# Feeding the filling work of the attention pipelines by an estimate of how far VectorE and ScalarE are behind TensorE

## The chip, the cores and the metric

The kernel runs on one core of one Trainium2 chip, as one launch. The metric is the device time of that core in microseconds (us). Engines are named PE (TensorE), DVE (VectorE), ACT (ScalarE), POOL (GpSimd) and SP (SyncE, which here issues transfers).

## The reference

Two layers of a transformer block over 512 image tokens `x` and 256 context tokens `z`, width 1024, everything in float32. Cut to what matters:

```
def hybrid_layer(x, z, c, c_ctx, p, ...):
    mod_x = silu(c) @ p['w_ada'] + p['b_ada']       # six vectors of 1024: shift, scale, gate, twice
    mod_z = silu(c_ctx) @ p['w_ada'] + p['b_ada']
    hx, hz = x * (1 + sc1x) + sh1x, z * (1 + sc1z) + sh1z
    mix_x, mix_z = token_mixers(hx, hz, ...)
    x = layer_norm(ALPHA * x + g1x * mix_x)
    x = layer_norm(ALPHA * x + g2x * sq_relu_mlp(x * (1 + sc2x) + sh2x))
    ...                                             # z likewise, in the first layer only

def token_mixers(hx, hz, p, ...):                   # three branches, each with its own projections
    ya = retention_branch(...)   # 4 heads, two directions, silu gates g_fwd and g_bwd
    yb = na_branch(...)          # neighbourhood attention, 8 heads
    yc = mla_branch(...)         # latent attention, 8 heads
    y = sigmoid(g0) * (ya @ w_branch_ret) + sigmoid(g1) * (yb @ w_branch_na) + sigmoid(g2) * (yc @ w_branch_mla)
    return y @ p['w_out']
```

The second layer returns only `x`, so it has no context outputs there.

## The kernel before, in words

Every float32 product is made of three matmuls on a high and a low part (`mm3`). So each weight, fetched as a block of 128 x 1024, is first split: ACT writes the high part (`hi_of`, L383), DVE the low part of the first 512 columns and POOL that of the other 512 (`lo_of`, L386). Weights rotate through three buffers, the projections' results through three PSUM banks (`pd`).

The program order of a layer is: MLA pipeline, neighbourhood attention pipeline (Natten), retention pipeline of the first two heads (`ret.run(0)`), all filling work that is left (`fill.rest()`), retention pipeline of the other two heads (`ret.run(1)`), together with two branch projections, then the third branch projection, the output projection, layer norm, and the MLP in eight parts. In the first layer the output projection goes in two rounds, `z` first and then `x`. The compiler's scheduler may move an instruction ahead of others on its engine, but on PE the instructions stand close to program order.

`pipeline(items, lags, want)` walks the attention items in stages: scores and softmax (s0), transposes (s1), weighted values (s2). After each stage it calls `fill.feed(want / 3)`, which gives credit in us of PE time and advances generators of other work until the credit is used up. A generator yields after each piece and says how much PE time it holds (`cost`, columns / 2400). A piece can be larger than the credit; then the credit is negative and nothing is fed until it has been earned back. `Fill` has two queues: `urgent` is work that the next item needs (keys and queries of the next head, the projections and values of Natten, the preparation of a retention pair), and `jobs` is work that is needed only later: `ret_gates` (24 tiles of 256 columns in the first layer, 16 in the second, in four groups that share two weights) and `gate_tiles` (24 weights, each for a tile of 512 columns and in the first layer one of 256 too). `feed` takes from `urgent` first. `finish(gen)` runs a generator to its end, without credit, when its result is needed.

A third stream hangs on the first. `later` (class `Paced`) holds the modulation vectors that are not yet there: 80 blocks of `w_ada`, each fetched (512 KB) and then multiplied and summed by DVE, once for `x` and once for `z` (L500). Its instructions are pinned behind the DVE instruction that stands before them in program order. It advances by a rate per us of other work:

```
fill.after = lambda c: later.step(c * ADA_GATES)    # L1665, 0.3 for each us that fill.rest() feeds
later.step(c * ADA_BRANCH)                          # L1689, 0.05 in the third branch
later.until(1 + 8)                                  # L1710, before the output projection
later.step(ADA_OUT)                                 # L1735, 0.3 for each weight after the third
later.until(1 + 24)                                 # L1737, before the layer norm of each round
```

The first advance only fetches, so `until(1 + 8)` stands for eight blocks: the vector that scales the output projection's results (L1719). The next sixteen scale and shift the layer norm's result. In the MLP the rate is 1.1 for each weight.

Of the kernel before, what the change touches and what calls it, by code (L numbers as in the profile page):

```python
# [42 lines left out]
WANT = ((4.0, 2.5, 6.0, 8.0), (4.0, 2.5, 6.0, 8.0))  # L43

RET_LAGS = ((0, 1, 3), (0, 1, 2))

NA_AHEAD = 2

# [11 lines left out]
class Units:  # L60


    def __init__(self):
        self.index = {}
        self.blocks = []
# [172 lines left out]
class Fill:  # L238
# [2 lines left out]

    def __init__(self):
        self.urgent = []
        self.jobs = []
        self.credit = 0.0
        self.after = None

    def step(self):  # L250
        for queue in (self.urgent, self.jobs):
            while queue:
                c = next(queue[0], None)
                if c is not None:
                    if self.after:
                        self.after(c)
                    return c
                queue.pop(0)
        return None

    def feed(self, want):
        self.credit += want
        while self.credit > 0:
# [3 lines left out]
                return  # L267
            self.credit -= c

    def finish(self, gen):  # L270
        if gen in self.urgent:
            self.urgent.remove(gen)
        for _ in gen:
            pass

    def rest(self):
        while self.step() is not None:
            pass


class Pending:
# [31 lines left out]
def block_kernel(ctx, tc, xT, zT, cond, wu, sp, bias, tab, out):  # L313
    nc = tc.nc
# [32 lines left out]
    def bank_d():  # L347

        return ps_d.tile([128, 512], F32, tag="pd", name=nm("pd"))
# [26 lines left out]
    def R(ap):  # L376
        return ap.bitcast(F32R)

    act, dve, pool, pe, sync = nc.scalar, nc.vector, nc.gpsimd, nc.tensor, nc.sync
    fill, pend = Fill(), Pending()  # L380

    def hi_of(dst, src, scale=1.0):
        act.activation(R(dst), src, AF.Copy, scale=scale)  # L383
# [25 lines left out]
    dve.memset(ones, 1.0 / D)  # L409


    def load(*key, spare=False):
        raw = dbl("wraw") if spare else wraw.tile([128, 1024], F32, tag="wraw", name=nm("wraw"))
        fetch_in(raw, wu[IDX[key]])
        return raw

    def weight(*key, own=False, spare=False, w_dve=W_DVE):
        raw = load(*key, spare=spare)
        if own:
            w = (dbl("w"), dbl("w"))  # L420
        else:
            t = wsp.tile([128, 2, 1024], F32, tag="wsp", name=nm("wsp"))
            w = (t[:, 0], t[:, 1])
        hi_of(w[0], raw)
        for eng, cols in ((dve, slice(0, w_dve)), (pool, slice(w_dve, 1024))):
            if cols.start < cols.stop:
                lo_of(w[1][:, cols], raw[:, cols], w[0][:, cols], eng)
        return w
# [273 lines left out]

        return s0, s1, s2

    def pipeline(items, lags, want, tick=None):

        n = len(items)
        for t in range(n + lags[-1]):  # L710
            for s, lag in enumerate(lags):
                if 0 <= t - lag < n:
                    items[t - lag][s]()
                fill.feed(want / len(lags))
            if tick:
                tick(t)

# [419 lines left out]
    def ret_gates(l, hx, hz, need, store):  # L1137
# [5 lines left out]
        for p2 in range(2):  # L1143
            for dr, name in enumerate(("gf", "gb")):
                wg = [weight(l, name, p2, j) for j in range(2)]
                for i, lhs in enumerate(tiles):
                    p = bank_d()[:, :256]
                    token_major(p, lhs, wg, 4, KT)
                    g = ft("gt")[:, :256]
                    act.activation(g, p, AF.Tanh, scale=0.5)  # L1150
                    dve.scalar_tensor_tensor(g, g, 1.0, p, ALU.add, ALU.mult)
                    sync.dma_start(store[p2, i][dr], g)
                    yield cost(24 * 256)

    class Retention:
# [260 lines left out]

        def run(self, p2, want):
            items = [self.item(p2, o, c) for o in range(2) for c in range(3 if self.need else 2)]
            pipeline(items, RET_LAGS[p2], want)


    def gate_tiles(l, groups, store):
# [446 lines left out]
```

## Time and profile before

| | us |
|---|---|
| timed runs: median of 3 (lowest to highest) | 2669.43 (2669.32 to 2672.81) |
| the profiled execution, device time | 2672.0 |
| its span, first to last instruction | 2670.0 |
| PE busy in the span | 2524.7 (95%) |
| DVE busy in the span | 1801.6 (67%) |

The span is what the trace covers; some 2 us lie around it. Stages are given as stretches of the span, in us from its start: MLA 115 to 410, Natten 410 to 607, `ret.run(0)` 607 to 687, what `fill.rest()` and the last credit of `ret.run(0)` feed 687 to 787, `ret.run(1)` and the branches 787 to 912, the output projection 912 to 989, all in the first layer; and MLA 1636 to 1880, Natten 1880 to 2049, `ret.run(0)` 2049 to 2114, the rest of the filling 2114 to 2160, in the second. Neighbouring stages overlap by a few us. "PE busy" of a stretch counts a matmul to its modelled end, so the time without a busy PE is the stretch less that number. PEclk is the granted share of TensorE's 2.4 GHz; 0.5 is 1.2 GHz.

### The profile page before, as it was taken

The numbers are of one execution on the slowest core, as the hardware profiler recorded it, in microseconds if no ns is written. First come the engines' busy times: TensorE is split into PE (matmuls) and PEld (weight loads), VectorE is DVE, ScalarE is ACT, GpSimd is POOL, SyncE is SP. The second block draws the span as 40 slices with busy tenths as digits, with TensorE's granted clock in tenths as the row PEclk, the third lists the DMA queues.
The fourth block names the chain that finished last, engine by engine and source line by source line (L and its number), as shares of the span: only waits on it lengthen the run. The fifth ranks groups of instructions, "written<-read, shape, count | busy, mean of one in ns | idle before, by whom it ended". The sixth has DMA issues, their size and how long they took to land. (4 is left out here: it accounts for less than half of the span.)

```text
span 2670.0 us, 40740 instructions
## 1 busy us (share of the span) xinstructions
PE 2524.7 (95%) x15218; PEld 2241.1 (84%) x15218; DVE 1801.6 (67%) x3326; ACT 1157.5 (43%) x2176; POOL 1048.8 (39%) x816
## 2 busy tenths in 40 slices
PE   6999999997999898999999989999999899999997
PEld 4899998987888787888888878888888788888887
DVE  8565556676978894767777775566568758734357
ACT  4555545563323345222222345555556434632225
POOL 6312113345335655222222452222334557743334
PEclk8999999999999999999999999999999999999999
DMA  6222223423665543344444423332342356433333
GB/s 237 72 87 83 72 85 95 141 78 98 237 205 153 191 127 103 111 133 125 134 134 122 133 83 114 96 96 88 117 149 91 103 185 206 127 111 95 98 100 119
DMA packets 143001, 329.48 MB, mean 123 GB/s; under 512 B 16978, under 2 KB 54738, under 8 KB 142804
## 3 DMA queue, kind: packets, MB, share of 16 engines
q1 hardware_dynamic: 132436, 311.15, 37.7%
q10 hardware_dynamic: 10368, 15.73, 1.6%
q8 instruction: 120, 1.97, 0.3%
q14 instruction: 77, 0.63, 0.1%
HBM read 288.27 MB, written 36.45 MB: 122 GB/s over the span
## 5 line engine op out<-in xcount | busy, mean ns | idle before, releaser
L432 PE MATMUL pd<-op,wsp 128*128 128x512 f32 (+1 forms) x3080 | 1074.8, 350 | 38.6 <-DVE ms L1492 8.4
L433 PE MATMUL pd<-op,wsp 128*128 128x512 f32 (+1 forms) x3080 | 1073.0, 348 | 14.6 <-DVE op L386 8.4
L434 PE MATMUL pd<-op,wsp 128*128 128x512 f32 (+1 forms) x3080 | 1069.3, 347 | 7.1 <-DVE wsp L386 7.1
L386 POOL TENSOR_TENSOR wsp<-wraw,wsp 128x512 fp32r<-128x512 f32 x317 | 522.3, 1650 | 988.3 <-ACT wsp L383 874.3
L432 PEld LDWEIGHTS pd<-op,wsp 128*128 128x128 f32 x3080 | 588.6, 192 | 115.8 <-ACT op L588 10.0
L433 PEld LDWEIGHTS pd<-op,wsp 128*128 128x128 f32 x3080 | 590.2, 192 | 87.7 <-DVE op L386 12.3
L434 PEld LDWEIGHTS pd<-op,wsp 128*128 128x128 f32 x3080 | 589.3, 191 | 80.1 <-DVE wsp L386 9.4
L383 ACT ACTIVATE wsp<-wraw 128x1024 fp32r<-128x1024 f32 x319 | 336.2, 1055 | 391.5 <-PE pd L434 271.1
L386 DVE TENSOR_TENSOR wsp<-wraw,wsp 128x512 fp32r<-128x512 f32 (+1 forms) x319 | 283.3, 889 | 190.7 <-ACT wsp L383 184.7
L647 PE MATMUL pd<-wsp,op 128*128 128x256 f32 x704 | 203.1, 289 | 2.5 <-DVE pr L757 2.0
L649 PE MATMUL pd<-wsp,op 128*128 128x256 f32 x704 | 201.3, 286 | 0.2 <-POOL wsp L386 0.2
L648 PE MATMUL pd<-wsp,op 128*128 128x256 f32 x704 | 201.1, 286 | 0.0
L500 DVE CUSTOM_DVE_ANT_0 cond<-graw,cond,sp 128x1024 bf16<-128x1024 f32 x112 | 167.5, 1495 | 43.3 <-DMA graw<-wu 42.8
L1756 DVE TENSOR_TENSOR rl<-rl 128x256 f32<-128x256 f32 (+1 forms) x104 | 68.6, 659 | 138.9 <-ACT rl L1755 138.6
L386 DVE TENSOR_TENSOR pt<-pst,pt 128x512 fp32r<-128x512 f32 (+1 forms) x208 | 121.3, 602 | 48.2 <-ACT pt L383 46.4
L647 PEld LDWEIGHTS pd<-wsp,op 128*128 128x128 f32 x704 | 137.1, 195 | 3.6 <-issue 2.8
L649 PEld LDWEIGHTS pd<-wsp,op 128*128 128x128 f32 x704 | 136.6, 194 | 0.8 <-POOL wsp L386 0.4
L648 PEld LDWEIGHTS pd<-wsp,op 128*128 128x128 f32 x704 | 137.0, 195 | 0.1
L1770 DVE TENSOR_TENSOR t<-pd,t 128x512 f32<-128x512 f32 (+1 forms) x132 | 80.4, 613 | 77.6 <-PE pd L434 77.4
L1755 ACT ACTIVATE rl<-pd 128x256 f32<-128x256 f32 (+1 forms) x104 | 51.6, 496 | 174.3 <-PE pd L434 174.2
L616 PE MATMUL pso<-pt,t 128*128 128x256 f32 x704 | 115.3, 293 | 10.7 <-DVE ntx L623 4.0
L383 ACT ACTIVATE pt<-pst 128x512 fp32r<-128x512 f32 (+1 forms) x208 | 104.8, 529 | 46.4 <-PE pst L599 39.8
(284 smaller groups left out, 3925.8 us busy)
## 6 DMA issues: line engine op xcount, KB each, us to landing
wraw<-wu SPq DMA_DIRECT2D x327, 512.0 KB, 3.7
graw<-wu SPq DMA_DIRECT2D x56, 512.0 KB, 3.7
ada<-wu SPq DMA_DIRECT2D x40, 512.0 KB, 5.7
gg<-gate ACTq DMA_DIRECT2D x48, 256.0 KB, 2.0
gl<-gg SPq DMA_DIRECT2D x48, 256.0 KB, 3.6
zbias<-bias SPq DMA_DIRECT2D x64, 128.0 KB, 2.3
t<-vd SPq DMA_DIRECT2D x28, 256.0 KB, 5.4
gd<-gt SPq DMA_DIRECT2D x40, 128.0 KB, 2.4
```

The lines of the kernel that those rows point to most:

```text
L383: act.activation(R(dst), src, AF.Copy, scale=scale)
L386: (eng or dve).tensor_tensor(R(dst), src, hi, op=ALU.subtract)
L432: pe.matmul(ps, R(a[0]), R(b[0]), start=start, stop=False)
L433: pe.matmul(ps, R(a[0]), R(b[1]), start=False, stop=False)
L434: pe.matmul(ps, R(a[1]), R(b[0]), start=False, stop=stop)
L500: i = dve.tensor_tensor_reduce(cs[2], raw, cs[t], 0.5, spt[l][:, SP_BADA + c : SP_BADA + c + 1], ALU.mult, ALU.add, mods[l][:, c, t : t + 1])
L616: pe.matmul(o, R(vts[k]), R(pts[k]), start=k == 0, stop=k == n - 1)
L647: pe.matmul(ps, R(a[0]), R(w[0][:, o : o + 256]), start=k == 0, stop=False)
L648: pe.matmul(ps, R(a[1]), R(w[0][:, o : o + 256]), start=False, stop=False)
L649: pe.matmul(ps, R(a[0]), R(w[1][:, o : o + 256]), start=False, stop=k == nk - 1)
L1756: dve.tensor_tensor(t, t, t, op=ALU.mult)
L1770: dve.tensor_tensor(a, ps, a, op=ALU.add)
```

## The change

Operations on ACT, DVE, POOL and PE are counted as the program is written out: `Metered` adds to `Load` a duration worked out from the columns of the operation's output, and `Load` keeps for each engine the time at which it would be through, with a start no earlier than 1.0 us (`EARLY`) before PE's own time. `behind()` is how far the later of ACT and DVE is past PE. After each stage of a pipeline, `fill.level()` advances generators of `jobs` (not `urgent`, and without credit) as long as `behind()` is over 2.0 us (`LEAD`). `ret.run(1)` has no levelling. While a group of `ret_gates` is unfinished (`holding`), `feed` too takes from `jobs` alone, and `finish` completes the group first. The function `load` is renamed `raw_weight`, since its name is used for the estimate.

```
--- before.py
+++ after.py
@@ -43,6 +43,8 @@
 WANT = ((4.0, 2.5, 6.0, 8.0), (4.0, 2.5, 6.0, 8.0))
 
 RET_LAGS = ((0, 1, 3), (0, 1, 2))
+
+LEAD, EARLY = 2.0, 1.0
 
 NA_AHEAD = 2
 
@@ -241,14 +243,17 @@
 
 
 
-    def __init__(self):
+    def __init__(self, load):
         self.urgent = []
         self.jobs = []
         self.credit = 0.0
         self.after = None
-
-    def step(self):
-        for queue in (self.urgent, self.jobs):
+        self.load = load
+
+        self.holding = False
+
+    def step(self, queues=None):
+        for queue in (self.jobs,) if self.holding else queues or (self.urgent, self.jobs):
             while queue:
                 c = next(queue[0], None)
                 if c is not None:
@@ -267,7 +272,15 @@
                 return
             self.credit -= c
 
+    def level(self):
+
+        while self.load.behind() > LEAD:
+            if self.step((self.jobs,)) is None:
+                return
+
     def finish(self, gen):
+        while self.holding:
+            self.step()
         if gen in self.urgent:
             self.urgent.remove(gen)
         for _ in gen:
@@ -276,6 +289,50 @@
     def rest(self):
         while self.step() is not None:
             pass
+
+
+class Load:
+
+
+
+
+
+    RATES = {"act": (0.15, 0.9e-3), "dve": (0.08, 1.15e-3), "pool": (0.1, 3.0e-3)}
+
+    def __init__(self):
+        self.pe = 0.0
+        self.end = dict.fromkeys(self.RATES, 0.0)
+
+    def add(self, name, out):
+        n = 1
+        for d in out.shape[1:]:
+            n *= d
+        if name == "pe":
+            self.pe += max(n / 2400.0 + 0.013, 0.11)
+        else:
+            fixed, column = self.RATES[name]
+            self.end[name] = max(self.end[name], self.pe - EARLY) + fixed + column * n
+
+    def behind(self):
+        return max(self.end["act"], self.end["dve"]) - self.pe
+
+
+class Metered:
+
+
+    def __init__(self, engine, name, load):
+        self.engine, self.name, self.load = engine, name, load
+
+    def __getattr__(self, op):
+        f = getattr(self.engine, op)
+        if op == "dma_start":
+            return f
+
+        def counted(out, *a, **k):
+            self.load.add(self.name, out)
+            return f(out, *a, **k)
+
+        return counted
 
 
 class Pending:
@@ -376,8 +433,10 @@
     def R(ap):
         return ap.bitcast(F32R)
 
-    act, dve, pool, pe, sync = nc.scalar, nc.vector, nc.gpsimd, nc.tensor, nc.sync
-    fill, pend = Fill(), Pending()
+    load = Load()
+    act, dve, pool, pe = (Metered(e, n, load) for e, n in ((nc.scalar, "act"), (nc.vector, "dve"), (nc.gpsimd, "pool"), (nc.tensor, "pe")))
+    sync = nc.sync
+    fill, pend = Fill(load), Pending()
 
     def hi_of(dst, src, scale=1.0):
         act.activation(R(dst), src, AF.Copy, scale=scale)
@@ -409,13 +468,13 @@
     dve.memset(ones, 1.0 / D)
 
 
-    def load(*key, spare=False):
+    def raw_weight(*key, spare=False):
         raw = dbl("wraw") if spare else wraw.tile([128, 1024], F32, tag="wraw", name=nm("wraw"))
         fetch_in(raw, wu[IDX[key]])
         return raw
 
     def weight(*key, own=False, spare=False, w_dve=W_DVE):
-        raw = load(*key, spare=spare)
+        raw = raw_weight(*key, spare=spare)
         if own:
             w = (dbl("w"), dbl("w"))
         else:
@@ -702,7 +761,7 @@
 
         return s0, s1, s2
 
-    def pipeline(items, lags, want, tick=None):
+    def pipeline(items, lags, want, tick=None, level=True):
 
 
 
@@ -712,6 +771,8 @@
                 if 0 <= t - lag < n:
                     items[t - lag][s]()
                 fill.feed(want / len(lags))
+                if level:
+                    fill.level()
             if tick:
                 tick(t)
 
@@ -1143,7 +1204,9 @@
         for p2 in range(2):
             for dr, name in enumerate(("gf", "gb")):
                 wg = [weight(l, name, p2, j) for j in range(2)]
+                fill.holding = True
                 for i, lhs in enumerate(tiles):
+                    fill.holding = i < len(tiles) - 1
                     p = bank_d()[:, :256]
                     token_major(p, lhs, wg, 4, KT)
                     g = ft("gt")[:, :256]
@@ -1416,7 +1479,7 @@
 
         def run(self, p2, want):
             items = [self.item(p2, o, c) for o in range(2) for c in range(3 if self.need else 2)]
-            pipeline(items, RET_LAGS[p2], want)
+            pipeline(items, RET_LAGS[p2], want, level=p2 == 0)
 
 
     def gate_tiles(l, groups, store):
```

## Rows read from the trace of the kernel before

**Rows 1.** The page: busy time by engine, then tenths in 40 slices.
```profile
PE 2524.7 (95%) x15218; PEld 2241.1 (84%) x15218; DVE 1801.6 (67%) x3326; ACT 1157.5 (43%) x2176; POOL 1048.8 (39%) x816
...
PE   6999999997999898999999989999999899999997
...
DVE  8565556676978894767777775566568758734357
```

**Rows 2.** Busy time by stage of the first layer: stretch, its length, engines, clock, DMA.
```profile
core 0: us, PE busy (x) PEld busy (x) DVE busy (x) ACT busy (x) POOL busy (x), PEclk, DMA share, GB/s
115.00:410.00 295.00, 293.81 (x2049) 272.75 (x2049) 175.36 (x347) 159.16 (x354) 63.65 (x51) 1.00 0.28 88
410.00:607.00 197.00, 187.35 (x1316) 172.09 (x1315) 139.91 (x323) 118.42 (x269) 73.86 (x79) 1.00 0.33 100
607.00:687.00 80.00, 64.89 (x428) 59.53 (x427) 53.71 (x152) 29.66 (x68) 44.71 (x44) 0.94 0.38 113
687.00:787.00 100.00, 98.40 (x573) 86.98 (x572) 87.78 (x151) 31.33 (x54) 26.95 (x19) 1.00 0.70 235
787.00:912.00 125.00, 116.04 (x684) 101.34 (x683) 95.26 (x219) 34.28 (x62) 67.72 (x58) 0.99 0.58 183
912.00:989.00 77.00, 71.85 (x417) 62.66 (x416) 72.99 (x107) 32.83 (x50) 44.40 (x35) 1.00 0.41 123
```

**Rows 3.** The same by stage of the second layer.
```profile
1636.00:1880.00 244.00, 240.30 (x1525) 216.14 (x1524) 147.42 (x272) 132.05 (x268) 57.13 (x39) 1.00 0.32 99
1880.00:2049.00 169.00, 164.32 (x1105) 149.19 (x1104) 110.57 (x251) 96.53 (x201) 69.29 (x74) 0.99 0.38 116
2049.00:2114.00 65.00, 55.67 (x360) 50.20 (x359) 52.33 (x138) 29.06 (x63) 36.94 (x36) 0.95 0.29 92
2114.00:2160.00 46.00, 42.78 (x184) 35.02 (x183) 21.62 (x34) 18.84 (x28) 17.96 (x14) 0.96 0.53 172
```

**Rows 4.** Gate tiles by stage, line 1434: MLA, end of the first filling, second layer.
```profile
L1434 ACT ACTIVATE gate<-pd x20: 363/490/602, 223.7 to 368.1; 128x512 f32<-128x512 f32 x10, 128x256 f32<-128x256 f32 x10
L1434 ACT ACTIVATE gate<-pd x24: 363/486/602, 686.8 to 783.9; 128x512 f32<-128x512 f32 x12, 128x256 f32<-128x256 f32 x12
L1434 ACT ACTIVATE gate<-pd x15: 597/597/597, 1706.0 to 1852.4; 128x512 f32<-128x512 f32 x15
L1434 ACT ACTIVATE gate<-pd x8: 581/598/598, 2114.4 to 2157.6; 128x512 f32<-128x512 f32 x8
```

**Rows 5.** Busy time of line 500 alone, by stage: stretch, length, DVE busy (instructions).
```profile
687.00:787.00 100.00, 56.60 (x80) 1.00 0.70 235
787.00:912.00 125.00, 3.78 (x4) 0.99 0.58 183
912.00:989.00 77.00, 18.59 (x20) 1.00 0.41 123
```

**Rows 6.** Line 500, minimum/median/maximum ns: 690 to 790, then 870 to 990.
```profile
L500 DVE CUSTOM_DVE_ANT_0 cond<-ada,cond,sp x40: 1271/1284/2325, 697.5 to 769.3; 128x1024 bf16<-128x1024 f32 x40
L500 DVE CUSTOM_DVE_ANT_0 cond<-ada,cond,sp x8: 1271/2130/2400, 890.5 to 945.7; 128x1024 bf16<-128x1024 f32 x8
```

**Rows 7.** Costliest DVE groups in the output projection, 912 to 989: busy us, mean ns.
```profile
L1719 DVE SCALAR_TENSOR_TENSOR t<-pd,mod,t 128x512 f32<-128x512 f32 x8 | 5.9, 742 | 0.7 <-PE pd L434 0.7
L1512 DVE TENSOR_TENSOR lnq<-lnq,lnt 128x512 f32<-128x512 f32 x6 | 5.7, 954 | 0.0
...
L1513 DVE TENSOR_TENSOR lns<-lns,t 128x512 f32<-128x512 f32 x4 | 3.7, 922 | 0.2
```

**Rows 8.** DVE groups of Natten, 410 to 607: busy us, mean ns.
```profile
L386 DVE TENSOR_TENSOR pt<-pst,pt 128x512 fp32r<-128x512 f32 x40 | 27.5, 686 | 5.1 <-ACT pt L383 4.7
...
L1073 DVE CUSTOM_DVE_ANT_0 p<-pss,zbias 128x512 f32<-128x512 f32 x32 | 21.6, 682 | 2.6 <-PE pss L675 2.5
...
L610 DVE TENSOR_SCALAR p<-p,tiny 128x512 f32<-128x512 f32 x32 | 17.1, 536 | 0.6
```

**Rows 9.** Around PE's longest wait, in the first `ret.run(0)`: columns as in rows 2.
```profile
653.00:660.00 7.00, 0.74 (x7) 0.53 (x5) 3.48 (x7) 2.50 (x6) 6.12 (x8) 0.89 0.00 0
660.00:667.00 7.00, 6.06 (x35) 6.09 (x36) 4.39 (x19) 0.89 (x3) 2.60 (x3) 0.63 0.06 18
```

## The prediction, made before the changed kernel was run

> **What bounds the kernel.** I read the page's busy times first, then busy time by stage for both layers, then where the gate tiles and the modulation blocks lie, then the durations of what would move. PE is busy 95% of the span and carries nearly the same work after the change, so only its idle time can change. DVE is next, busy 67% on average, but not evenly [rows 1]. In the two attention pipelines of the first layer PE is idle for 295 - 293.8 = 1.2 us (MLA) and 197 - 187.4 = 9.7 us (Natten); in the second layer 3.7 and 4.7 us. The two `ret.run(0)` leave 15.1 and 9.3 us [rows 2, 3]. So levelling has at most 19.3 us to win in MLA and Natten, and 24.4 us in `ret.run(0)`. The reader is to see two more things. From 687 to 787 PE is busy for 98.4 of 100 us, and so is DVE for 87.8 [rows 2]: 56.6 us of that are modulation blocks [rows 5], which this stretch of filling hides completely. And in the output projection, 912 to 989, DVE is busy for 73.0 of 77 us, more than PE with 71.9 [rows 2]. There DVE has no room.
>
> **How much filling the estimate takes early.** I went through the stages in program order with the constants of `RATES`, the columns of each operation and the queue rules, before and after the change, and summed what `jobs` yields, in the generators' own unit (`cost`). In the first layer there are 24 x 2.56 + 24 x 7.68 = 245.8 us of it. By the old rules 138.2 are used by the end of MLA, 153.6 by the end of Natten, 174.1 by the end of `ret.run(0)`, and 71.7 are left for `fill.rest()`. The trace agrees: 20 gate tiles lie in MLA, and the last 24 of 48 after 686 us (five by the last credit, 19 by `fill.rest()`) [rows 4].
>
> By the new rules 176.6 are used by the end of MLA, 235.5 by the end of Natten, all 245.8 in the first steps of `ret.run(0)`, and **nothing is left** for `fill.rest()`. In MLA levelling takes three tiles (12.8 us), and groups of gates that `finish` must now complete take the other 25.6. In Natten it takes ten (41 us). One item shows why: its s0 adds 0.67 + 0.08 + 0.67 = 1.42 us to DVE and 4 x 0.12 = 0.48 to PE, its s1 0.67 and 0.44, its s2 0.19 on average and 0.48, so the estimated lag grows by 0.9 us an item unless something is fed. Its urgent pieces are 7.7 to 15.4 us long against a credit of 2.5 an item, so for three to six items nothing is. The rates aren't far off: 0.67 us is estimated where 686 and 682 ns were measured, though 536 for L610 [rows 8]. With the threshold anywhere from 1.5 to 3.0 us, 2.6 us at most are left for `fill.rest()`. In the second layer 163.8 us are used up by the end of Natten, where before 25.6 were left for `fill.rest()`; it has no modulation.
>
> **What that does to the modulation.** `later` gets its 0.3 per us from `fill.rest()` alone. Before: 71.7 x 0.3 = 21.5 advances, 20 blocks after the first, and line 500 has 40 instructions there [rows 6]. After: none. The third branch (30.7 us of `cost` x 0.05) gives one or two. So `until(1 + 8)` forces some seven blocks at once before the output projection, whose evacuations need them, and `until(1 + 24)` some fourteen at once before the layer norm of `z`, on which the MLP's first matmuls wait. Pinned behind the DVE instruction before them, they can't start earlier. Twenty blocks thus move from 687-787 into 912-989.
>
> **The sum**, from the profiled execution's 2672.0 us:
>
> 1. *The forced blocks.* A block is two L500, two short reads and mostly one small operation. It took 56.6 / 20 = 2.8 us in the filling stretch and 18.6 / 5 = 3.7 us in the output projection [rows 5]. I take 3.0, nearer the first, since a starved PE leaves POOL and ACT idle too. DVE then has 73.0 + 20 x 3.0 = 133 us to do in a stretch of 77. Of that, the `x` statistics (5.7 + 3.7 us [rows 7]) can come after the layer norm of `z`. 124 - 77 = **+47**. Bounds: with 3.7 a block and nothing put off +70; with 2.8 and 25 us put off (also the evacuations of `x` and some of its weights) +27. In SP's queue 20 x 512 KB come on top of 123 GB/s x 77 us = 9.5 MB: 20 MB in 124 us, 161 GB/s, under the 235 of the filling stretch [rows 2], so transfers set no longer time. Queued behind a block on DVE are the low parts of the next weights and the evacuations, and PE has three banks and three weights to run ahead.
> 2. *Waits filled in MLA and Natten.* I take half of 19.3: **-10** (0 to -19). A wait for a result already in flight goes if a gate tile stands before it, but a late tile with its own splits can make another.
> 3. *`ret.run(0)`.* In the first layer some 10 us of gates come in its first steps: **-3** (0 to -8). In the second there is nothing left to level with: 0.
> 4. *The rest taken out.* Its gate work only changes place (its matmuls, one weight transfer and three splits a tile pair): 0 on PE; MLA and Natten have DVE 59 to 71% busy [rows 2, 3] and take it. But `ret.run(1)` now follows at once, with DVE's estimated debt at 11 and 9 us where it was none, and only the branch projections as cover: **+6** (0 to +20).
> 5. The Python classes issue nothing: 0. The second layer's `gate` stores, on ACT's queue, are earlier: 0.
>
> 47 - 10 - 3 + 6 = +40: 2712 for an execution like the profiled one. The runs' median is 2.6 us lower: **2709 us**, and this case's own range is 2680 to 2750.
>
> **Two rules of the Trainium skill.** L500 takes 1284 ns at the median in the filling stretch and 2130 in the third branch and output projection [rows 6], where POOL is busier (58% against 27% [rows 2]). "GPSIMD Engine Reference", Specifications, says that POOL shares its SBUF interfaces with VectorE and contends with DVE instructions that have two SBUF inputs, as L500 and the weights' splits have. By that rule a forced block costs the higher price as long as POOL works beside it, and term 1 is near its upper end; by the rows alone it is what I took.
>
> A wait of 7 us in `ret.run(0)` was followed by a stretch with PEclk at 0.63, that is, partly at 1.2 GHz [rows 9]. "TensorE: Matmul & The Clock Gate", HAM oscillation, says that a PE which keeps running dry falls back to the low clock again and again. By that rule a burst costs more than the DVE work in it, which is the third rival below.
>
> **Rivals.**
>
> *A, faster: the filling lasts.* If levelling triggers less than I worked out (or the scheduler places it so that little is drawn), gates remain for `fill.rest()`. Each us left brings 0.3 block, 0.9 us of DVE, back under cover. The gain of terms 2 and 3 (13 us) wins as soon as 47 - 0.9 x left is under 13, that is from 38 us left, five pairs of 24. With 52 or more left nothing is forced and the time is 2669 - 13 = 2656. For it: a count that slips in one queue rule. Against: no threshold that I tried leaves more than 2.6 us.
>
> *B, the same: the burst is absorbed.* The scheduler may put evacuations and splits between the blocks while their 512 KB land, and PE runs on through the `x` projection. But the layer norm of `z` needs all 24 blocks, so DVE's sum stands; only if also the blocks cost 2.8 us, 25 us are put off and terms 2 and 3 reach their ends does it come to 27 - 27 = 0: 2669.
>
> *C, slower still: the clock.* If PE is at 1.2 GHz through the whole burst, its 71.9 us become 144, more than DVE's 124, and term 1 is +67: 2729.
>
> **How the numbers follow.** Chances: forecast 0.65, A 0.15, B 0.10, C 0.10. The range goes from A's 2656 to a little under the forecast's own upper end, which takes in C: 2655 to 2745. A measurement of this kernel can tell 0.2%, 5 us, from no change. Faster: A without its middle, and half of B's lower side, 0.17. Same: 0.07. Slower: 0.76.
>
> **What would show it.** In the changed profile: gate tiles (L1434's counterpart) all before the end of `ret.run(0)`, and no stretch of gates alone; some 20 of the modulation's DVE instructions fewer before the third branch's end than the 40 shown; in the output projection DVE near 100% and PE waiting for evacuations behind modulation blocks, tens of us in two lumps, one before its first results and one before the layer norm of `z`; less PE idle in Natten; the MLP unchanged. What would make me wrong: gates left after `ret.run(0)`; blocks found in Natten or `ret.run(1)`; or an output projection of about 77 us as before.

## The result, and the profile after

The changed kernel takes 2756.78 us (median of 5 runs, 2752.31 to 2758.43), the kernel before 2670.22 us (5 runs beside it, 2669.32 to 2673.72). The ratio is 1.0321, 95% interval 1.0307 to 1.0335: 3.2% slower, by 86.6 us. The direction was forecast. The size was not: +39 us was predicted, and 2756.78 lies above the range's end of 2745.

The changed kernel's page, with the same three lines as [rows 1]:

```profile
PE 2541.1 (92%) x15218; PEld 2253.4 (82%) x15218; DVE 1794.7 (65%) x3326; ACT 1158.8 (42%) x2176; POOL 1054.8 (38%) x816
...
PE   6999999999969768999999989999999878999997
...
DVE  8455565557577997477677884656556788834357
```

The instruction counts are the same on every engine, so nothing was added; only the order differs. PE's tenths have new dips between the 12th and the 16th slice (69 us each) and one at the 33rd. Here every engine operation has one line, that of `Metered`'s helper, so the rest is read by tiles.

Stages of two kernels can be laid side by side only if they are cut at the same instructions. I cut at MLA's first copy of keys (`kt`), the last of its results for `x` (`tx`), the first elementwise product of retention (`pf<-pss`), the last `ry` of `ret.run(1)`, the first evacuation of the output projection, the MLP's first relu, and again in the second layer. Lengths in us so cut (Natten to the first `pf`; retention is `ret.run(0)`, `fill.rest()` and `ret.run(1)`):

```
                      first layer                                 second layer
             MLA    Natten  retention 3rd br.  output pr. MLP     MLA    Natten  retention out
before       286.6  199.1   261.8     49.3     69.3       657.2   245.6  168.8   153.4     30.2
changed      325.7  244.1   190.1     46.1     127.3      653.8   255.8  195.6   130.7     32.2
difference   +39.1  +45.0   -71.7     -3.2     +58.0      -3.4    +10.2  +26.8   -22.7     +2.0
gate tiles   +10    +11     -21                                   +3     +5      -8
```

The differences add up to +80, the two spans differ by 2750.5 - 2670.0 = 80.5. (Three tiles of `ret_gates`, 72 matmuls x 120 ns = 8.6 us, come before the cut between the first layer's MLP and the second's MLA in the changed kernel, and behind it in the kernel before: like for like these two are -12.0 and +18.8.) Busy time by stage of the changed kernel (columns as in [rows 2]):

```profile
123.00:448.00 325.00, 323.54 (x2202) 298.26 (x2202) 174.41 (x340) 162.82 (x358) 68.17 (x55) 1.00 0.28 89
448.00:692.00 244.00, 235.80 (x1587) 216.06 (x1587) 147.94 (x332) 130.46 (x289) 86.64 (x88) 0.99 0.33 103
692.00:883.00 191.00, 157.45 (x979) 142.06 (x978) 135.35 (x376) 63.86 (x130) 97.25 (x85) 0.89 0.44 132
883.00:929.00 46.00, 41.94 (x261) 37.22 (x259) 37.65 (x52) 13.79 (x22) 30.95 (x25) 1.00 0.83 287
929.00:1056.00 127.00, 83.01 (x354) 67.54 (x355) 115.31 (x190) 30.58 (x47) 45.92 (x31) 0.76 0.37 127
...
1966.00:2161.00 195.00, 187.07 (x1214) 167.69 (x1213) 126.30 (x262) 103.22 (x210) 71.87 (x73) 1.00 0.37 114
2161.00:2292.00 131.00, 99.40 (x551) 86.61 (x550) 101.56 (x256) 47.52 (x93) 71.14 (x63) 0.86 0.43 134
```

and of the kernel before, cut at the same instructions, the two retention stages:

```profile
609.00:870.00 261.00, 239.31 (x1464) 213.51 (x1463) 204.51 (x475) 81.62 (x161) 110.81 (x97) 0.98 0.55 175
...
2061.00:2214.00 153.00, 139.03 (x731) 118.61 (x730) 107.36 (x262) 59.40 (x109) 83.02 (x67) 0.97 0.45 142
```

The reader is to take two numbers from each row: length less PE busy, and DVE busy. In the output projection (929 to 1056) PE is idle for 44 us, DVE busy for 115 of 127. In the retention stages PE's idle time has grown, from 21.7 to 33.6 us in the first layer and from 14.0 to 31.6 in the second, though the stages are shorter. In MLA and Natten of the first layer it is 1.5 and 8.2 us: the changed kernel didn't win the 11 us that stood idle there.

Where the gate tiles went, by stage: MLA, Natten, retention, second layer's MLA and Natten ([rows 4] for before):

```profile
L333 ACT ACTIVATE gate<-pd x30: 384/492/601, 200.4 to 406.9; 128x512 f32<-128x512 f32 x15, 128x256 f32<-128x256 f32 x15
...
L333 ACT ACTIVATE gate<-pd x14: 362/492/601, 461.2 to 686.4; 128x512 f32<-128x512 f32 x7, 128x256 f32<-128x256 f32 x7
...
L333 ACT ACTIVATE gate<-pd x4: 384/492/599, 692.0 to 722.6; 128x512 f32<-128x512 f32 x2, 128x256 f32<-128x256 f32 x2
...
L333 ACT ACTIVATE gate<-pd x18: 597/599/601, 1747.6 to 1923.7; 128x512 f32<-128x512 f32 x18
...
L333 ACT ACTIVATE gate<-pd x6: 599/599/600, 1983.7 to 2079.5; 128x512 f32<-128x512 f32 x6
```

The third row's tile of 692.0 had its matmuls in Natten, which makes 15 there. The last tile of the first layer stands at 722.6, before the end of `ret.run(0)`; nothing is left for `fill.rest()` in either layer. A pair of tiles holds 24 x 227 ns + 24 x 120 ns = 8.33 us of matmuls, a single one of 512 columns 5.45 (from one matmul's start to the next in the trace).

The modulation's instructions (L500 of before, [rows 6]) from 880 to 1056:

```profile
L333 DVE CUSTOM_DVE_ANT_0 cond<-ada,cond,sp x48: 1268/1273/2315, 920.1 to 1021.3; 128x1024 bf16<-128x1024 f32 x48
L333 DVE CUSTOM_DVE_ANT_0 cond<-graw,cond,sp x4: 1271/1514/2309, 1030.8 to 1052.2; 128x1024 bf16<-128x1024 f32 x4
```

52 instructions are 26 blocks, all after 920.

What PE waited for in the output projection (925 to 1056), then in the first layer's retention (692 to 883), then in the second's (2161 to 2292): sum, times, longest.

```profile
PE pd L333 <- DVE wsp L333: 23.9, 7, 9.9
...
PE pd L333 <- DVE t L333: 9.5, 4, 3.9
...
PE pss L333 <- POOL tiny L333: 6.5, 1, 6.5
...
PE pso L333 <- DVE ry L333: 17.8, 2, 16.7
PE pd L333 <- ACT op L333: 5.9, 1, 5.9
...
PE pso L333 <- DVE ry L333: 14.2, 2, 13.4
PE pd L333 <- DVE ra L333: 6.9, 1, 6.9
PE pso L333 <- DVE ro L333: 6.5, 1, 6.5
```

The kernel before has the same instructions, and in its two retention stages (609 to 870, 2061 to 2214) PE waits far less for them:

```profile
PE pso L1402 <- DVE ry L1407: 1.6, 1, 1.6
...
PE pso L1402 <- DVE ry L1407: 4.0, 2, 3.2
```

In the output projection the low parts of the weights (`wsp`) and the evacuations (`t`) stand on DVE behind modulation blocks. PE's longest wait there, and DVE just before it ends:

```profile
942.27 10.61 PE L333 MATMUL pd<-op,wsp 128*128 128x256 f32 x70 [9.91 <-DVE wsp L333]
...
940.33 1.27 DVE L333 CUSTOM_DVE_ANT_0 cond<-ada,cond,sp 128x1024 bf16<-128x1024 f32 x1
...
941.53 0.68 DVE L333 TENSOR_TENSOR wsp<-wraw,wsp 128x512 fp32r<-128x512 f32 x1
```

In retention PE waits for `ry`, the evacuation of transposed results, at the end of `ret.run(0)`, with no other work on PE. The timeline of PE shows the longest such hole:

```profile
770.38 0.38 PE L333 MATMUL pso<-ctab,ro 128*128 128x128 f32 x2
787.47 0.69 PE L333 MATMUL pso<-ctab,ro 128*128 128x128 f32 x2 [16.71 <-DVE ry L333]
789.29 0.69 PE L333 MATMUL pso<-ctab,ro 128*128 128x128 f32 x2 [1.13 <-DVE ry L333]
795.89 2.38 PE L333 MATMUL pd<-op,wsp 128*128 128x512 f32 x4 [5.92 <-ACT op L333]
```

DVE is busy for 15.3 us of this hole. Until 779.4 it works on the last items' results (`ro`). Then comes the preparation of the second pair of heads (`st`, `qc`, `op`), and only behind it `ry`, though the transposes of 770.38 that it evacuates were long through:

```profile
778.95 0.41 DVE L333 TENSOR_TENSOR ro<-ro 128x256 f32<-128x256 f32 x1
779.39 1.93 DVE L333 TENSOR_TENSOR st<-t,st 64x256 fp32r<-64x256 f32 x3
781.35 2.72 DVE L333 TENSOR_TENSOR qc<-ra,qd 64x512 f32<-64x512 f32 x3
784.09 1.39 DVE L333 TENSOR_TENSOR op<-qc,op 64x512 fp32r<-64x512 f32 x2
...
786.93 0.48 DVE L333 TENSOR_SCALAR ry<-pso,sp 128x256 f32<-128x256 f32 x1
```

The second layer's 13.4 us end in the same order on DVE (2219.8 to 2228.2). Before, gate tiles stood at this place (686.8 to 783.9 in [rows 4]): DVE was as busy, and so was PE.

```profile
686.00:703.00 17.00, 15.40 (x93) 13.44 (x92) 15.73 (x34) 7.49 (x14) 7.64 (x7) 1.00 0.51 184
```

### The profile page after: what moved, and what is told of

It reads as the page before. It is cut to its first block, busy times and chain, and to the rows that moved or that the text cites. A ratio compares the mean times of both kernels' runs of the same rounds, so it can differ in the third digit from the quotient of the medians.

```text
span 2750.5 us, 40716 instructions
## 1 busy us (share of the span) xinstructions
PE 2541.1 (92%) x15218; PEld 2253.4 (82%) x15218; DVE 1794.7 (65%) x3326; ACT 1158.8 (42%) x2176; POOL 1054.8 (38%) x816
## 5 line engine op out<-in xcount | busy, mean ns | idle before, releaser
L333 PE MATMUL pd<-op,wsp 128*128 128x512 f32 (+1 forms) x9240 | 1775.0, 351 | 87.7 <-DVE wsp L333 28.1
L333 PEld LDWEIGHTS pd<-op,wsp 128*128 128x128 f32 x9240 | 1490.2, 193 | 316.7 <-DVE wsp L333 32.6
L333 PE MATMUL pd<-wsp,op 128*128 128x256 f32 x2112 | 268.7, 286 | 2.3 <-DVE pr L333 1.7
L333 PEld LDWEIGHTS pd<-wsp,op 128*128 128x128 f32 x2112 | 261.3, 194 | 3.7 <-issue 2.8
L333 DVE TENSOR_TENSOR t<-pd,t 128x256 f32<-128x256 f32 (+2 forms) x200 | 108.1, 546 | 85.4 <-PE pd L333 73.2
L333 PE MATMUL pso<-pt,t 128*128 128x256 f32 x704 | 116.5, 295 | 10.4 <-DVE ntx L333 3.2
L333 DVE CUSTOM_DVE_ANT_0 cond<-ada,cond,sp 128x1024 bf16<-128x1024 f32 x72 | 118.9, 1652 | 0.5
L333 PE MATMUL pst<-ctab,p 128*128 128x128 f32 x704 | 102.0, 274 | 10.0 <-DVE p L333 7.4
L333 PEld LDWEIGHTS pso<-pt,t 128*128 128x128 f32 x704 | 95.8, 192 | 16.4 <-DVE tz L333 3.3
L333 PEld LDWEIGHTS pst<-ctab,p 128*128 128x128 f32 x704 | 80.3, 140 | 19.2 <-DVE p L333 8.2
L333 POOL TENSOR_TENSOR op<-mh,op 128x256 fp32r<-128x256 f32 (+1 forms) x64 | 79.3, 1253 | 43.6 <-DVE mh L333 20.8
```

Source lines behind the costliest of these rows:

```text
L333: return f(out, *a, **k)
```

## The experiments

Two theories stood against each other. **The burst**: the loss is the modulation blocks, forced into the output projection. **The drain**: the gate work was the cover of the retention pipelines' ends, and its loss costs time of its own, blocks or none. Ratios are to the kernel before, timed in the same session.

**1. The changed kernel, nine (first layer) and five (second) gate weights held back until `fill.rest()`.** `gate_tiles` gets a slice of its weights; the rest of the change stays.

```
+KEEP = (9, 5)
-        fill.jobs.append(gate_tiles(l, groups, g_mix))
+        fill.jobs.append(gate_tiles(l, groups, g_mix, slice(0, 24 - KEEP[l])))
...
             fill.after = lambda c: later.step(c * ADA_GATES)
+        fill.jobs.append(gate_tiles(l, groups, g_mix, slice(24 - KEEP[l], 24)))
         fill.rest()
```

> The changed kernel, but the last 9 gate weights of the first layer and the last 5 of the second are held back from levelling and credit until fill.rest(), about what the kernel before leaves there. Theory 'cover lost' (the time is lost because fill.rest() runs empty; levelling itself costs nothing): 2655 to 2675. Rival 'levelling costs' (the order that levelling and the held gate groups make in MLA and Natten is itself slower): 2690 or more.

Measured: 2694.47 us, 1.0075 (1.0051 to 1.0099). The lump went (output projection 73.2 us), yet 22 us remain: the theory's figure was missed, and the rival's holds. By the cuts the second layer lost nothing (-1); like for like, with three tiles of `ret_gates` before its cut, it lost 7 and the first layer's MLP gave 8 back. MLA took all 30 tiles that it could have, and Natten got none:

```profile
124.00:450.00 326.00, 324.56 (x2207) 299.02 (x2206) 175.39 (x341) 163.50 (x359) 69.03 (x55) 1.00 0.29 89
450.00:646.00 196.00, 185.70 (x1288) 170.45 (x1287) 141.35 (x326) 118.12 (x268) 73.95 (x80) 0.98 0.32 95
```

Natten is 196.0 us with no tile, where before it was 199.1 with four, which hold 16.7. So 13.6 us are lost there, and another 9 in retention, which has six tiles (25 us) less and is 16 us shorter. Filling taken from a stage is not given back in full by that stage.

**2. The kernel before, MLA's credit raised so that the gates are gone before `fill.rest()`.** No levelling.

```
-WANT = ((4.0, 2.5, 6.0, 8.0), (4.0, 2.5, 6.0, 8.0))
+WANT = ((6.2, 2.5, 6.0, 8.0), (5.4, 2.5, 6.0, 8.0))
```

> The kernel before, without any levelling, whose MLA pipeline is fed 6.2 and 5.4 us an item in place of 4.0, so that by the queue rules nothing is left for fill.rest() in either layer. Theory 'cover lost': 2740 to 2770, as slow as the changed kernel, with the same lump in the output projection. Rival 'levelling costs': 2665 to 2685, since nothing is levelled.

Measured: 2758.11 us, 1.0314 (1.0290 to 1.0338), as slow as the changed kernel; MLA holds 43 of the 48 tiles, and the output projection takes 124.7 us. Nothing of the loss needs the estimate: an empty `fill.rest()` is enough. The retention stages show the drain here too, with nothing levelled or held: 24 tiles less (100 us) shorten the first layer's by 80.3, eight less (43.6) the second's by 24.3.

**3 and 4. The changed kernel and the kernel before, without the arithmetic of `later`'s blocks.** Both leave out the product and sum of these blocks: each result is a constant 0.5, and their fetches stay.

```
-            modulation(*u, raws[i], cs, True)
+            tc.keep_in_program_order(dve.memset(mods[u[0]][:, u[1], :], 0.5))
```

> The changed kernel, with the arithmetic of the 80 later modulation blocks left out: each block is still fetched, but in place of its two multiply-and-sum instructions and the adjustment stands one memset of its two columns to 0.5 (so layer norms and gates use 0.5). Theory 'cover lost': the output projection of the first layer loses its lump, 58 us by the trace of the changed kernel (from its first evacuation to the MLP's first, 127 us against 69), while the wait at the end of ret.run(0) stays: 2690 to 2705. Rival 'not the blocks' (PE's clock or the drain of the retention pipelines sets the loss): 2735 or more.

> The kernel before with the same arithmetic left out. Theory 'cover lost': the blocks are hidden there but for some waits in the MLP (up to 20 us idle in front of evacuations): 2650 to 2668, so that e3 less e4 is 25 to 45 us, against 87 between the kernels with the blocks. Rival 'not the blocks': e3 less e4 is 70 or more.

Measured: 2707.34 us, 1.0122 (1.0097 to 1.0147), and 2661.08 us, 0.9950 (0.9930 to 0.9970). Without a block on DVE, 46 of the 87 us are still there, a little more than both figures allowed (2705, and 45 between the two). The profiled executions differ by 53.5 us, of which 4.6 come before MLA; by them the loss lies behind the output projection (+29, second layer above all), in the output projection (+15) and in the first layer's attention (+5). The 15 go with transfers, as far as the waits tell: the output projection of the changed order, without blocks, is 88 us long at 292 GB/s,

```profile
930.00:1018.00 88.00, 73.05 (x390) 63.00 (x389) 57.10 (x109) 32.17 (x50) 42.37 (x32) 0.90 0.80 292
```

and SP's queue issues thirteen fetches of 512 KB in a row, for 13.26 us, between two of weights:

```profile
937.19 3.58 SPq L451 DMA_DIRECT2D wraw<-wu  x2
940.85 13.26 SPq L597 DMA_DIRECT2D ada<-wu  x13
955.12 2.88 SPq L451 DMA_DIRECT2D wraw<-wu  x3
```

PE waits 10.4 us there for the high parts of weights, 7.2 of them at once. The three weights of 955.12 landed 10.1 us after their issue, where 4.0 is the median in the same stretch of experiment 4. But ACT went to their splits straight from the layer norm's operations, so how much of the 15 the late landing costs isn't separated. The burst is also sharper here than in the changed kernel, where fetches wait for DVE to have read a block (26.1 us, five times, from 880 to 1056).

**5. The changed kernel, all of `later`'s blocks computed from one resident block.** 79 transfers are left out, and DVE's work is all there; from the second block on it multiplies the first block again.

```
-                t = dbl("ada") if i < roomy else graw.tile([128, 1024], F32, tag="graw", name=nm("graw"))
-                sync.dma_start(t, wu[IDX[units[i][0], "ada", units[i][1]]])
-                raws.append(t)
+                if not raws:
+                    t = graw.tile([128, 1024], F32, tag="graw", name=nm("graw"))
+                    sync.dma_start(t, wu[IDX[units[i][0], "ada", units[i][1]]])
+                raws.append(raws[0] if raws else t)
```

> The changed kernel, but the 80 later modulation blocks are all multiplied with one block that is fetched once; the other 79 transfers of 512 KB are left out, and the modulation vectors come out other than the reference's. DVE's work is unchanged. Theory 'DVE': the lump in the output projection is DVE's time, so from its first evacuation to the MLP's first it still takes 112 to 127 us, and the whole 2735 to 2755. Rival 'transfers' (the forced fetches hold up the weights in SP's queue; without the arithmetic that stretch still took 83 us against 68): 85 to 100 us there, the whole 2705 to 2730.

Measured: 2748.23 us, 1.0292 (1.0277 to 1.0307). The output projection is still 118.8 us long, so of its 58 us 49.5 are DVE's time and 8.5 go with the transfers:

```profile
933.00:1051.00 118.00, 78.74 (x352) 65.10 (x353) 113.42 (x191) 30.61 (x46) 47.98 (x30) 0.77 0.21 66
```

**6. The change in the second layer only**, which has no modulation: `level` and `holding` act when `l == 1`.

```
-        while self.load.behind() > LEAD:
+        while self.levels and self.load.behind() > LEAD:
...
+        fill.levels = l == 1
```

> The changed kernel with levelling and held groups in the second layer alone; the first layer is fed as before. Theory 'drain': a retention pipeline without gate work behind it costs time with no modulation at hand, as the second layer's 16 us in the changed trace say: 2682 to 2692. Rival 'blocks alone' (all of the loss hangs on the first layer's modulation): 2666 to 2674.

Measured: 2694.03 us, 1.0093 (1.0077 to 1.0110), +24 us: the drain, 2 us above its figure. MLA, Natten and retention of the second layer:

```profile
1655.00:1910.00 255.00, 249.94 (x1517) 221.33 (x1516) 144.61 (x267) 133.30 (x266) 62.54 (x49) 1.00 0.33 103
1910.00:2107.00 197.00, 189.24 (x1220) 170.10 (x1219) 127.14 (x264) 103.63 (x211) 72.04 (x73) 0.99 0.36 113
2107.00:2239.00 132.00, 98.65 (x548) 85.82 (x548) 101.49 (x255) 47.37 (x93) 70.99 (x63) 0.87 0.43 133
```

Natten, with its step into retention, grew by 27.6 us for five tiles that hold 27.2. Retention lost eight tiles (43.6 us) and is only 21.5 us shorter.

**7. The changed kernel, levelling with dummy work.** `level` feeds 24 matmuls of 256 columns with no weight, no splits and no store instead of gate tiles; no `holding`, no levelling in retention. All gates stay where they were. It adds 24 such groups, 576 matmuls x 120 ns = 69 us; what comes back is what levelling fills.

```
         while self.load.behind() > LEAD:
-            if self.step((self.jobs,)) is None:
-                return
+            self.extra()
```

> The kernel before, with levelling in MLA and Natten of both layers that doesn't take from the jobs: each time the estimate is over 2.0 us, 24 extra matmuls of 256 columns go into a PSUM bank that nothing reads. That is 24 times 24 matmuls, 24 x 2.88 = 69 us of PE at 120 ns each, with no DVE, ACT or transfer behind it. If a fill at these places takes waits away as term 2 of the prediction has it (10 of 19 us), the kernel grows by 59 or less; theory 'waits not filled' (PE's waits there are not where the estimate fires, or come back elsewhere): by 64 to 74.

Measured: 2721.22 us, 1.0191 (1.0176 to 1.0206), +51.5, on the side of filled waits by the total. But the levelled stages say otherwise: first layer +7.6 (MLA) and +24.3 (Natten), second +5.7 and +26.6, 64 of the 69 us. The missing 12 us come from the first layer's MLP (645.7 us against 657.2), where nothing is levelled. PE's idle time shows it too; the four stages:

```profile
120.00:414.00 294.00, 293.61 (x2060) 273.32 (x2059) 171.59 (x338) 156.15 (x346) 63.66 (x51) 1.00 0.25 83
414.00:638.00 224.00, 217.13 (x1567) 202.73 (x1567) 142.87 (x328) 121.26 (x273) 77.01 (x82) 1.00 0.29 91
1661.00:1912.00 251.00, 247.39 (x1566) 222.51 (x1565) 145.93 (x271) 132.17 (x266) 60.18 (x45) 1.00 0.30 97
1912.00:2108.00 196.00, 190.18 (x1330) 176.14 (x1329) 116.75 (x259) 96.70 (x201) 69.52 (x72) 0.99 0.32 101
```

16.7 us are idle where 19.1 were before, cut in the same way. The estimate puts its filling at places where PE hardly waits.

**8. Levelling in `ret.run(0)` only**, no `holding`, both tiles of a gate weight as one piece.

```
-        pipeline(items, (0, 1, 2), want, tick)
+        pipeline(items, (0, 1, 2), want, tick, level=False)
...
-            pipeline(items, (0, 1, 3), want)
+            pipeline(items, (0, 1, 3), want, level=False)
...
-                    yield cost(24 * n)
+                yield cost(24 * sum(n for _, n in groups))
```

> The changed kernel with levelling in ret.run(0) alone, in both layers, no held groups, and a gate weight's two tiles fed as one piece. MLA and Natten then use what they used before, and ret.run(0), where PE waits 15 and 9 us, has gate work to level with. Theory 'cover lost' (filling is worth most where a retention pipeline would wait, and the rest stays for fill.rest()): fill.rest() is shorter by what is drawn, some blocks are forced; 2655 to 2680. Rival 'levelling costs': 2690 or more.

Measured: 2703.26 us, 1.0123 (1.0106 to 1.0140), in the rival's range. Here PE does wait, and levelling does fill: with the same 24 tiles, retention of the first layer is 248.5 us instead of 261.8. But the larger pieces make MLA and Natten 10 us longer with the same tiles, the blocks are forced (output projection 103.4, +34), and the second layer loses 7.

**9. As 8, first layer only, with the blocks advanced by the gate work of `ret.run(0)` too**, so that none need be forced.

```
-                    if self.after:
+                    if self.after and queue is self.jobs:
...
-        ret.run(0, want[2])
-        fill.finish(preps[1])
         if l == 0:
             fill.after = lambda c: later.step(c * ADA_GATES)
+        ret.run(0, want[2])
+        fill.finish(preps[1])
         fill.rest()
```

> As e10_level_ret0_only, but levelled in the first layer alone, and the gate work that is fed in ret.run(0) advances the modulation at the same 0.3 per us as in fill.rest(), so that no block is forced. Theory 'cover lost': the lump of 34 us that e10 has in the output projection is gone, and the 9 us that levelling wins in the retention pipelines stays: 2655 to 2668, faster than the kernel before. Rival (the blocks only move: DVE has no room for them in ret.run(0), where it is 67% busy): 2672 to 2690.

Measured: 2734.01 us, 1.0231 (1.0215 to 1.0248): both figures were missed. The lump is gone (output projection 70.8), and retention is 327.3 us instead of 261.8. From 617 to 854:

```profile
617.00:854.00 237.00, 163.36 (x963) 144.92 (x962) 142.22 (x313) 54.76 (x106) 77.07 (x59) 0.85 0.43 140
...
L333 DVE CUSTOM_DVE_ANT_0 cond<-ada,cond,sp x48: 1269/1285/1845, 637.4 to 804.2; 128x1024 bf16<-128x1024 f32 x48
```

The gate tiles are through by 724.7, the blocks run on to 816, and retention's own DVE operations stand behind them: PE waits 22.7 us at a time for `ktf` and 15.7 for `pf`. The blocks' DVE time moves with whatever feeds them; of the stretches tried, only that of gate tiles alone hides it.

**10. The kernel before, its blocks forced**, with all gate work where it was: the first term of the sum alone.

```
-ADA_GATES = 0.3
+ADA_GATES = 0.0
```

> The kernel before with ADA_GATES = 0: all gate work stays where it was, but fill.rest() no longer advances the modulation, so the same blocks are forced before and in the output projection as in the changed kernel. This measures the forced blocks alone. By term 1 of the prediction: +47, 2717; by the changed kernel's trace: +58, 2728. Rival 'drain first' (the lump is so large only because DVE comes to it with the retention pipelines' debt): +35 or less, 2705 or less.

Measured: 2717.39 us, 1.0170 (1.0146 to 1.0194), +44 us; output projection 126.0 us (+57), with the changed kernel's picture:

```profile
918.00:1044.00 126.00, 82.99 (x358) 67.72 (x359) 114.94 (x190) 31.05 (x48) 45.47 (x30) 0.76 0.36 123
```

**11 and 12. Levelling in `ret.run(0)` with gates held back for `fill.rest()`**, experiment 8 with the slices of experiment 1: in the first layer only, then in both.

```
+KEEP = (9, 0)
-            pipeline(items, RET_LAGS[p2], want, level=p2 == 0)
+            pipeline(items, RET_LAGS[p2], want, level=p2 == 0 and self.l == 0)
```

> As e10_level_ret0_only, but levelled in the first layer alone, and with the last 9 gate weights held back until fill.rest(), where 69 us of cost advance the modulation by 20 blocks as before; levelling in ret.run(0) can draw three weights. Theory 'cover lost': no lump in the output projection (69 to 75 us there), and the 9 us that e10 wins in the retention pipelines: 2658 to 2667. Rival 'moved, not won' (what levelling fills in ret.run(0) is missing behind it): 2668 to 2680.

> The same in both layers, the second with its last 5 gate weights held back. Theory 'cover lost': the second layer adds up to 5 us of gain to e13: 2653 to 2665. Rival 'moved, not won': within 5 us of e13, or slower than it, as e10's second layer was by 7 us.

Measured, with 12 runs against 23 of before: 2671.76 us, 1.0010 (0.9999 to 1.0021), and 2673.21 us, 1.0016 (1.0004 to 1.0028). Both gains that were expected are missed, and the rival's figures hold. In the first of the two the retention stage of the first layer takes 260.3 us, MLA and Natten are 11 us longer (larger pieces again), and up to the MLP the kernel is 12 us behind; the total is level only because the first layer's MLP takes 644.8 us instead of 657.2. No version with all of the kernel's work beats the kernel before.

## Why the prediction was right in direction and wrong in size

**The count of the filling: right.** 30 tiles in MLA are 15 weights, 176.6 us of gate work with the rest of the queue, as worked out; Natten nearly finishes it, `ret.run(0)` starts the last tiles in its first steps, and `fill.rest()` has nothing. Rival A is out, and with it the whole lower part of the range; so is rival B, since forced blocks alone cost 44 us (experiment 10).

**Term 1, the forced blocks (+47): right in mechanism, and in its total partly by luck.** Forced alone they cost 44 us (experiment 10), and DVE sets most of that time (experiment 5). 26 blocks lie in the stretch from 920 instead of the five of [rows 5]. DVE's sum came out: for this cut the term makes it 66.2 (before, 920 to 989) + 60 - 9.4 = 116.8 us, and it is 115.3. But DVE is also idle for 11.7 of the 127 us, so the stretch grew by 57 to 58 us, not by 47. I had said that transfers set no time; 8.5 us of the 58 go with them (experiment 5). The total agrees because the first layer's MLP gives 9 us back in experiment 10, which no term held.

By the rule of "GPSIMD Engine Reference", Specifications, in the Trainium skill, that POOL contends with DVE instructions that have two SBUF inputs, the forced blocks would have been dear. That did not decide here: though single ones took up to 2315 ns, the 48 took 1273 ns at the median, the lower price of [rows 6], with POOL busy for 36% of the stretch. Rival C was half right. The granted clock fell to 0.76, as the Trainium skill's "TensorE: Matmul & The Clock Gate", HAM oscillation, lets one expect of a PE that keeps running dry, and PE was busy 83.0 us for what took 64.0 before. But DVE with 115.3 of 127 us set the time, and the lower clock was hidden under it.

**Term 4, the rest taken out (+6, 0 to +20): this is the step that failed.** I took the gate tiles' matmuls to be worth the same wherever they stand, and saw only a debt of some us on DVE. The runs show that the end of `ret.run(0)`, where DVE works through the last items and the second pair's preparation, needs other work on PE beside it, and that retention loses about 20 us in each layer without (17 and 21 here, 20 and 19 in experiment 2). In the second layer 43.6 us of gate work were taken out and 22.7 came back (21.5 in experiment 6, where this alone costs +24). The stage's rows account for it: PE's idle time rose by 17.6 us, and its busy time is 99.4 where 139.0 - 43.6 = 95.4 would be left at the old clock (PEclk 0.97 before, 0.86 after). In the first layer 21 tiles less are 88.8 us, and 71.7 came back; there idle time rose by 11.9 us, and PE was busy 157.5 us for 239.3 - 88.8 = 150.5, with PEclk at 0.89 instead of 0.98. Term 3's -3 is swallowed in this. With the third branch (-3.2) and the second layer's output projection (+2.0), terms 3 and 4 together are 17.1 + 20.9 - 3.2 + 2.0 = **+37**, not +3.

**Term 2, the waits filled in MLA and Natten (-10): nearly nothing.** The tiles cost what they hold. In the first layer ten are 41.7 us where MLA grew by 39.1, and eleven are 47.1 where Natten grew by 45.0; in the second three are 16.4 where MLA grew by 18.8 (like for like), and five are 27.2 where Natten grew by 26.8. That is -2.7 in all. Experiment 7 agrees: levelling with work that needs nothing else fills some 5 of 69 us there.

**The sum, as measured.** By stages: +58.0 for the output projection, +37 for terms 3 and 4, -2.7 for term 2 and -12.0 for the first layer's MLP, which makes the +80 of the profiled execution. By runs: forced blocks 44 (experiment 10), second layer 24 (experiment 6), and some 9 in the first layer up to its third branch (39.1 + 45.0 - 71.7 - 3.2) make 77 of 87 us; the other 10 are less than what the first layer's MLP varies. Both theories hold: the burst for about half of the loss, the drain for some 33 us.

**What stays open.** The first layer's MLP is 645 to 657 us long, like for like, from kernel to kernel with the same 108 modulation instructions inside (645.7 in experiment 7, 648.2 in 10, 644.8 in 11); no run isolates why. So a total within some 12 us isn't settled by the totals alone. Of the first layer's drain, the 16.7 us for `ry` and the 5.9 for the branch operands' `op` are seen, not separated. That the DVE work ahead of `ry` sets the hole is read from the timelines; no run shortened it, or put `ry` ahead of the second pair's preparation.

**What the profile was to show.** Tiles before the end of `ret.run(0)`, a full DVE and waits in the output projection: as said, though in many waits (the longest 9.9 and 6.5 us) and not two lumps. Less PE idle in Natten: 8.2 us where 9.7 were. Before the third branch's end 39 of the modulation's DVE instructions are missing, five where 44 were; the 20 of the forecast are blocks, of two instructions each. The MLP was to be unchanged, and is 12.0 us shorter like for like.

## What to carry to other kernels

Work that stands idle in a queue may be the cover of something later: before feeding it earlier, list what runs under it now (here the modulation on DVE, and the tails of two pipelines) and price each as if the cover were gone. Filling pays only where PE waits, so read the idle time of the stage that is to be filled first: two stages with 99% and 95% PE could return 11 us at most, and the kernel that lost its cover to them is 87 us slower. On the side of the estimate, a lag that is computed from the program's order says nothing of whether PE has other work ready.

## What the runs showed of the hardware

Two things I had not expected. In experiment 3 the fetches of 512 KB on one queue moved 409 GB/s from 930 to 965, above every stretch of [rows 2] (235 at most), and the three weights queued behind thirteen of them landed 10.1 us after their issue instead of some 4. And a stretch with long waits costs twice: in the second layer's retention the granted clock went from 0.97 to 0.86, so PE's own work there took 4 us more than the matmuls that left would explain. Around the first layer's hole of 16.7 us, from 770 to 800, the granted clock was 0.54, close to the lower of its two levels (0.5 is 1.2 GHz).
